# Attention in units of both heads and half a group's queries, the third score product on half the array's rows

## The chip, the cores and the metric

The kernel runs on one core of a Trainium2 chip. The time is the device time of one execution in microseconds (us). The engines of the core run side by side: TensorE (PE in the rows; its weight loads are a second row, PEld), VectorE (DVE), ScalarE (ACT), GpSimd (POOL), and SyncE (SP), which issues the DMAs. Matmuls write into PSUM, eight banks of 512 fp32 columns on 128 partitions; ACT and DVE read them from there.

## The reference

Two layers over 2048 tokens of width 1024. Layer 0 is a gated linear attention; layer 1, which the change touches, is a stick-breaking attention with 16 heads of 64 dimensions. Its core, per head and query:

```python
z = q @ k.T * scale                                   # keys strictly before the query
log_beta = log_sigmoid(z)
log_one_minus = where(strictly_before, log_beta - z, 0)
log_survive = cumsum(log_one_minus, reverse) - log_one_minus
weights = where(strictly_before, exp(log_beta + log_survive), 0)
o = (weights @ v) * silu(g) ; x + gate * (o @ w_out)
```

## The kernel before

All products are made in fp32r from a high and a low part of each operand, three matmuls for one product. Tokens lie in four groups of 512 (TG). Layer 0 takes the first 970 us or so of the span. Layer 1 runs over eight pairs of heads (p), and within a pair over the four query groups (g). For each pair and group `pair_linear` makes k, q, v and the gate g from the normed tokens (96 matmuls and more).

**Scores.** k holds, for each head, the high part in one half of the 128 partitions and the low part in the other. q's high part stands in both halves, so one 128-row matmul gives high times high and high times low (L821). The low part of q, also copied into both halves, gives the third product, with low times low for free (L822). Sigmoid of the scores on ACT (L825) gives 1 - beta; on a diagonal block POOL masks it (L827); a backward running product on DVE (L830) gives the survival of the stick, in S.

**Turns and values.** Four transposes (L838) bring a column block of S into a PSUM bank `pt`, of which there are two (pool `pw`). ACT takes the high part out of it (L841, `sh`), DVE the low part (L842, `sl`). Since S runs as a product, the values are multiplied as differences of neighbours, in high and low parts side by side (`v2`); two matmuls (L855, L856) add a turned block into the bank `o`. At the end `finish` adds the halves and multiplies by the gate.

**Units.** A unit is one head h, one query group g and one key group c (c from g down to 0). It has four steps: the four blocks of 128 queries for the scores, and the four blocks of 128 keys for turns and values. A diagonal unit (c = g) has shorter rows in both. TensorE's order is the order of the code (`manual_schedule`): at each step a score call, a share of the side work (`fill`: the next `pair_linear`, or the last projection), the values of a block turned three steps before, and the turn of a block whose scores began five steps before (LAG_T, LAG_V). The order on ACT and DVE is the scheduler's. The next pair's weights are scaled and split by ACT and DVE (`load_scaled`) during the third group of a pair and the fourth.

**q.** After its projection q's high part goes into half the partitions of `L.q` on ACT, one head at a time (L776, L777), its low part to `ql` on DVE (L778, L780), and four DMAs copy them into the other halves (L783, L784). 

The call that sets the order of the steps:

```python
u.scores(j)
turns.append((u, j))
step(fill, (i + 0.7) / len(steps))
if len(values) > LAG_V: ...          # values of an earlier turn
if len(turns) > LAG_T: ...           # a turn
```

Of the kernel before, what the change touches and what calls it, by code (L numbers as in the profile page):

```python
# [9 lines left out]
F32 = mybir.dt.float32  # L10
F32R = mybir.dt.float32r
AF = mybir.ActivationFunctionType
ALU = mybir.AluOpType
# [21 lines left out]
def yoco_kernel(ctx: ExitStack, tc: tile.TileContext, I: dict, O: dict):  # L35
# [696 lines left out]
    def pair_linear(p, g, W, Ls):  # L732
# [23 lines left out]
        else:  # L756
# [21 lines left out]
        nc.vector.scalar_tensor_tensor(L.ql[0][A], pq[A], bq[A], L.q[A, 0].bitcast(F32),  # L778
                                       op0=ALU.add, op1=ALU.subtract)
        nc.vector.scalar_tensor_tensor(L.ql[1][B], pq[B], bq[B], L.q[B, 1].bitcast(F32),  # L780
                                       op0=ALU.add, op1=ALU.subtract)
# [19 lines left out]
    class Unit:  # L801
# [6 lines left out]
        def __init__(self, p, g, h, c, Ls, before):  # L808
            self.p, self.g, self.h, self.c = p, g, h, c
            self.Ls, self.before = Ls, before  # L810
            self.diag = c == g
            self.n = f"{p}_{g}_{h}_{c}"
            self.S, self.split = [], []

        def scores(self, tb):
            L, h, diag = self.Ls[self.g], self.h, self.diag
            k = self.Ls[self.c].k
            w = (tb + 1) * P if diag else TG
# [4 lines left out]
            s_ = t2(f"S_{self.n}_{tb}")  # L823
            s = s_[:, 0:w]
            nc.scalar.activation(s, z, AF.Sigmoid, scale=-SCALE_B)  # L825
            if diag:
                nc.gpsimd.affine_select(s[:, w - P:], s[:, w - P:], pattern=[[-1, P]],  # L827
                                        compare_op=ALU.is_gt, fill=1.0, base=0, channel_multiplier=1)

            nc.vector.tensor_tensor_scan(s[:, ::-1], s[:, ::-1], s[:, ::-1],  # L830
                                       1.0 if diag else self.before.S[tb][:, 0:1], ALU.mult, ALU.min)
            self.S.append(s_)

        def turn(self, sb):
            t0 = sb if self.diag else 0
            pt = bank(pw, f"pt_{self.n}_{sb}")
            for tb in range(t0, 4):
                nc.tensor.transpose(pt[:, tb * P:(tb + 1) * P], self.S[tb][:, sb * P:(sb + 1) * P], ident)  # L838
            hi = t2(f"sh_{self.n}_{sb}", F32R)[:, t0 * P:]
            lo = t2(f"sl_{self.n}_{sb}", F32R)[:, t0 * P:]  # L840
            nc.scalar.activation(hi, pt[:, t0 * P:], AF.Copy, bias=-1.0)  # L841
            nc.vector.scalar_tensor_tensor(lo, pt[:, t0 * P:], -1.0, hi.bitcast(F32),  # L842
                                           op0=ALU.add, op1=ALU.subtract)
            self.split.append((hi, lo))

        def values(self, sb):
            if self.diag and sb == 0:
                self.o = bank(po, f"o_{self.n}")
            elif sb == 0:
                self.o = self.before.o  # L850
            t0 = sb if self.diag else 0
            o = self.o[:, t0 * P:]
            v = self.Ls[self.c].v[:, sb, self.h].rearrange("p a d -> p (a d)")
            hi, lo = self.split[sb]
            nc.tensor.matmul(o, v, hi, start=self.diag and sb == 0, stop=False)  # L855
            nc.tensor.matmul(o, v, lo, start=False, stop=self.c == 0 and sb == 3)  # L856
            if self.c == 0 and sb == 3:
                self.finish()

        def finish(self):  # L860
            p, g, h = self.p, self.g, self.h
            L = self.Ls[g]
            mine = slice(64 * h, 64 * h + 64)
            other = slice(64 - 64 * h, 128 - 64 * h)
            if h == 0:
                L.o = t2(f"oB_{p}_{g}")
            tmp = t2(f"ot_{p}_{g}_{h}")
            nc.scalar.activation(tmp[mine], self.o[other], AF.Copy)
            nc.vector.tensor_tensor(L.o[mine], self.o[mine], tmp[mine], op=ALU.add)  # L869
            if h == 1:  # L870
                nc.vector.tensor_tensor(L.o, L.o, L.g, op=ALU.mult)
# [60 lines left out]
    def layer1(after):  # L932
        Ls = {p: [] for p in range(SBP)}
        weave(pair_linear(0, 0, Ws[0], Ls[0]), (after, 0, 2))
        turns, values = [], []
# [28 lines left out]
        for p in range(SBP):  # L964
            for g in range(NG):
                units = []
                for h in range(2):
                    before = None
                    for c in range(g, -1, -1):
                        before = Unit(p, g, h, c, Ls[p], before)  # L970
# [102 lines left out]
```

## Time and profile before

| | |
|---|---|
| Time, median of 3 runs | 2706.01 us (2699.67 to 2706.11) |
| The profiled execution | 2703.88 us, of which the span of the program is 2702.1 us |
| TensorE busy | 2607.2 us, 96% of the span, 14040 matmuls |
| DVE busy | 2110.4 us, 78% |
| ACT busy | 1517.6 us, 56% |
| POOL busy | 167.4 us, 6% |
| DMA | 371.91 MB, 138 GB/s in the mean |

Busy times are unions of the instructions' times on one engine. A matmul's duration goes on after the next one has begun, so for TensorE the distance of two starts says what a matmul costs, and its duration says less. fp32 matmuls stand in the trace as two records each.

### The profile page before, as it was taken

The page shows a single profiled execution, that of the slowest core. Times are in us where ns is not written, and L with a number is a line of the kernel's source. Part 1 is how long each engine was busy: PE and PEld are TensorE (multiplying, and loading weights), DVE is VectorE, ACT ScalarE, POOL GpSimd, SP SyncE. Part 2 cuts the span into 40 slices and gives each one's busy share as a digit, 9 for nine tenths or more (in the row PEclk, how much of TensorE's full clock was granted, in tenths as well). Part 3 has the DMA queues.
Part 4 walks back from the last instruction along what each step waited for, and adds up shares of the span by engine and source line. Part 5 has one row for each costly group of instructions (what it writes and reads, how often), then busy time and mean ns, then how long its engine had stood idle before and what let it go on. Part 6 is the DMA issues. An engine that isn't in the chain of part 4 may idle for free.

```text
span 2702.1 us, 38165 instructions
## 1 busy us (share of the span) xinstructions
PE 2607.2 (96%) x14040; PEld 2184.4 (81%) x14040; DVE 2110.4 (78%) x2933; ACT 1517.6 (56%) x2677; POOL 167.4 (6%) x358
## 2 busy tenths in 40 slices
PE   5999999999999999999999999999999999999998
PEld 4888888888788878788787887887887887887887
DVE  7647767676675658978979969979879789789866
ACT  4746756574485445545545645546556555556644
POOL 3000000000000011000010010010000010010000
PEclk7999999999999999999999999999999999999999
DMA  6326445545732463342243334243243243323464
GB/s 246 118 74 209 151 151 175 168 148 173 232 131 72 164 247 127 106 145 90 96 146 116 114 107 154 88 137 116 75 148 110 72 151 113 115 93 117 148 212 147
DMA packets 116682, 371.91 MB, mean 138 GB/s; under 512 B 13872, under 2 KB 18096, under 8 KB 116496
## 3 DMA queue, kind: packets, MB, share of 16 engines
q1 hardware_dynamic: 116496, 369.47, 40.8%
q8 instruction: 111, 1.82, 0.3%
q14 instruction: 75, 0.61, 0.1%
HBM read 311.75 MB, written 40.89 MB: 131 GB/s over the span
## 4 chain that ended last, share of the span: by engine, by line
PE 75%; DVE 17%; ACT 3%; issue 3%; DMA 1%; POOL 0%; SPq 0%; DVEq 0%; POOLq 0%; ACTq 0%
PE pt L838 7%; DVE S L830 5%; PE z L822 4%; PE o L856 4%; PE z L821 4%; PE o L855 3%; DVE sl L842 3%; PE pg L150 2%; PE pg L152 2%; PE pg L151 2%; PE pf L150 2%; PE pf L151 2%; PE pf L152 2%; PE py L150 2%; PE lk L150 2%
## 5 line engine op out<-in xcount | busy, mean ns | idle before, releaser
L841 ACT ACTIVATE sh<-pt 128x512 fp32r<-128x512 f32 (+3 forms) x640 | 341.5, 534 | 531.7 <-PE pt L838 522.1
L842 DVE SCALAR_TENSOR_TENSOR sl<-pt,sh 128x512 fp32r<-128x512 f32 (+3 forms) x640 | 384.0, 601 | 163.5 <-ACT sh L841 157.6
L830 DVE TENSOR_TENSOR_SCAN S<-S,S 128x512 f32<-128x512 f32 x384 | 489.5, 1275 | 3.4 <-ACT S L825 3.0
L838 PE MATMUL pt<-ident,S 128*128 128x128 f32 x2176 | 346.9, 275 | 34.7 <-DVE sl L842 34.2
L838 PEld LDWEIGHTS pt<-ident,S 128*128 128x128 f32 x2176 | 266.1, 141 | 119.7 <-DVE sl L842 33.0
L825 ACT ACTIVATE S<-z 128x512 f32<-128x512 f32 (+3 forms) x640 | 339.5, 531 | 12.6 <-PE o L856 4.6
L821 PE MATMUL z<-k,q 128*128 128x512 f32 (+3 forms) x640 | 284.4, 444 | 0.0
L822 PE MATMUL z<-k,ql 128*128 128x512 f32 (+3 forms) x640 | 234.1, 366 | 0.9 <-DVE sl L842 0.5
L856 PE MATMUL o<-sl,v 128*128 128x512 f32 (+3 forms) x640 | 234.2, 366 | 0.0
L855 PE MATMUL o<-sh,v 128*128 128x512 f32 (+3 forms) x640 | 230.6, 360 | 0.0
L830 DVE TENSOR_TENSOR_SCAN S<-S 128x128 f32<-128x128 f32 (+3 forms) x256 | 209.3, 820 | 19.7 <-POOL S L827 16.7
L827 POOL TENSOR_SCALAR_AFFINE_SELECT S<-S 128x128 f32<-128x128 f32 x256 | 86.1, 337 | 1251.1 <-ACT S L825 1232.2
L444 PE MATMUL pv<-wh_v,h 128*128 128x256 f32 x512 | 155.0, 303 | 0.0
L446 PE MATMUL pv<-wh_v,h 128*128 128x256 f32 x512 | 145.3, 284 | 0.0
L445 PE MATMUL pv<-wl_v,h 128*128 128x256 f32 x512 | 145.2, 284 | 0.0
L855 PEld LDWEIGHTS o<-sh,v 128*128 128x128 f32 x640 | 120.6, 188 | 27.2
L856 PEld LDWEIGHTS o<-sl,v 128*128 128x128 f32 x640 | 120.6, 189 | 25.7
L821 PEld LDWEIGHTS z<-k,q 128*128 128x128 f32 x640 | 121.8, 190 | 5.5
L822 PEld LDWEIGHTS z<-k,ql 128*128 128x128 f32 x640 | 123.1, 192 | 1.5 <-DVE sl L842 0.7
L150 PE MATMUL pg<-h,wh_g 128*128 128x512 f32 x256 | 112.6, 440 | 0.0
L150 PE MATMUL lk<-xb,wh_w_kv 128*128 128x512 f32 x256 | 102.5, 400 | 7.6 <-DVE oB L869 7.6
L150 PE MATMUL lv<-xb,wh_w_kv 128*128 128x512 f32 x256 | 102.9, 402 | 3.5 <-DMA xb<-xn 3.5
(266 smaller groups left out, 6350.3 us busy)
## 6 DMA issues: line engine op xcount, KB each, us to landing
xb<-xn SPq DMA_DIRECT2D x256, 512.0 KB, 5.0
wa_l<-in_w_ada_dram SPq DMA_DIRECT2D x40, 512.0 KB, 5.2
wr_f<-in_w_out_dram SPq DMA_DIRECT2D x40, 512.0 KB, 3.8
x<-in_x_dram SPq DMA_DIRECT2D x32, 512.0 KB, 6.5
wr_v<-in_w_v_dram SPq DMA_DIRECT2D x32, 512.0 KB, 4.5
wr_kq<-in_w_kq_dram SPq DMA_DIRECT2D x32, 512.0 KB, 4.1
wr_g<-in_w_g_dram SPq DMA_DIRECT2D x32, 512.0 KB, 3.9
wr_out<-in_w_out_dram SPq DMA_DIRECT2D x32, 512.0 KB, 3.8
```

The costliest lines, as they stand in the source:

```text
L150: nc.tensor.matmul(out, hi, x[kt][0], start=first and i == 0, stop=False)
L444: nc.tensor.matmul(o, xh, hi, start=i == 0, stop=False)
L446: nc.tensor.matmul(o, xl, hi, start=False, stop=i == len(steps) - 1)
L821: nc.tensor.matmul(z, L.q[:, h, tcol], k[:, h, 0:w], start=True, stop=False)
L822: nc.tensor.matmul(z, L.ql[h][:, tcol], k[:, h, 0:w], start=False, stop=True)
L825: nc.scalar.activation(s, z, AF.Sigmoid, scale=-SCALE_B)
L830: nc.vector.tensor_tensor_scan(s[:, ::-1], s[:, ::-1], s[:, ::-1], 1.0 if diag else self.before.S[tb][:, 0:1], ALU.mult, ALU.min)
L838: nc.tensor.transpose(pt[:, tb * P:(tb + 1) * P], self.S[tb][:, sb * P:(sb + 1) * P], ident)
L841: nc.scalar.activation(hi, pt[:, t0 * P:], AF.Copy, bias=-1.0)
L842: nc.vector.scalar_tensor_tensor(lo, pt[:, t0 * P:], -1.0, hi.bitcast(F32), op0=ALU.add, op1=ALU.subtract)
L855: nc.tensor.matmul(o, v, hi, start=self.diag and sb == 0, stop=False)
L856: nc.tensor.matmul(o, v, lo, start=False, stop=self.c == 0 and sb == 3)
```

## The change

A unit is now both heads, half a query group (hf: 256 queries) and one key group.

- A score call takes 128 queries of both heads: two first products into two banks, then two third products. The third product of a head has only 64 rows: q's low part times k's high part, head 0 on array rows 0 to 63, head 1 on rows 64 to 127. It is called every second step, with two banks, two sigmoids and two scans; before, there was one of each at every step.
- A turned block has 128 keys, and both heads with 256 queries each. A value product is four matmuls, high and low for each head, of 256 columns. A diagonal unit of the first half has only two blocks of keys.
- q's high part is taken out of its bank in one operation of 128 partitions, its low part in another; four DMAs make `L.q`. There are no copies of the low part.
- A unit's end has two half-wide sums on ACT and DVE each, and half a gate, at the end of each half.

```diff
-        L.ql = [t2(f"ql{h}_{n}", F32R) for h in range(2)]
-        nc.scalar.activation(L.q[A, 0], pq[A], AF.Identity, bias=bq[A])
-        nc.scalar.activation(L.q[B, 1], pq[B], AF.Identity, bias=bq[B])
...
-        for x in (L.q[:, 0], L.q[:, 1]), L.ql:
-            nc.sync.dma_start(x[0][B].bitcast(F32), x[0][A].bitcast(F32))
-            nc.sync.dma_start(x[1][A].bitcast(F32), x[1][B].bitcast(F32))
+        qh, L.ql = t2(f"qh_{n}", F32R), t2(f"ql_{n}", F32R)
+        nc.scalar.activation(qh, pq, AF.Identity, bias=bq)
+        nc.vector.scalar_tensor_tensor(L.ql, pq, bq, qh.bitcast(F32), op0=ALU.add, op1=ALU.subtract)
+        for h, x in enumerate((A, B)):
+            for y in (A, B):
+                nc.sync.dma_start(L.q[y, h].bitcast(F32), qh[x].bitcast(F32))
...
-            z = bank(pz, f"z_{self.n}_{tb}")[:, 0:w]
-            nc.tensor.matmul(z, L.q[:, h, tcol], k[:, h, 0:w], start=True, stop=False)
-            nc.tensor.matmul(z, L.ql[h][:, tcol], k[:, h, 0:w], start=False, stop=True)
+            z = [bank(pz, f"z_{self.n}_{j}_{h}")[:, 0:w] for h in range(2)]
+            for h in range(2):
+                nc.tensor.matmul(z[h], L.q[:, h, tcol], k[:, h, 0:w], start=True, stop=False)
+            for h, rows in enumerate((A, B)):
+                nc.tensor.matmul(z[h], L.ql[rows, tcol], k[rows, h, 0:w], start=False, stop=True)
...
+            for h in range(2):
+                for j in range(f, 2):
+                    at = (2 * h + j) * P
+                    nc.tensor.transpose(pt[:, at:at + P], self.S[h, j][:, sb * P:(sb + 1) * P], ident)
...
-            nc.tensor.matmul(o, v, hi, start=self.diag and sb == 0, stop=False)
-            nc.tensor.matmul(o, v, lo, start=False, stop=self.c == 0 and sb == 3)
+            for h in range(2):
+                v = self.Ls[self.c].v[:, sb, h].rearrange("p a d -> p (a d)")
+                for i, x in enumerate(self.split[sb]):
+                    nc.tensor.matmul(self.o[:, h, f * P:], v, x[:, h], start=start and h == i == 0,
+                                     stop=stop and h == i == 1)
...
+            for h, (mine, other) in enumerate(((A, B), (B, A))):
+                nc.scalar.activation(tmp[mine], o[other, h], AF.Copy)
+                nc.vector.tensor_tensor(L.o[mine, cols], o[mine, h], tmp[mine], op=ALU.add)
+            nc.vector.tensor_tensor(L.o[:, cols], L.o[:, cols], L.g[:, cols], op=ALU.mult)
...
-                    u.scores(j)
-                    turns.append((u, j))
+                    if j % 2 == 0:
+                        u.scores(j // 2)
+                    sb = j + u.turns - 4
+                    if sb >= 0:
+                        turns.append((now + LAG_T, u, sb))
...
-                    if len(turns) > LAG_T:
-                        t = turns.pop(0)
+                    if turns and turns[0][0] <= now:
+                        t = turns.pop(0)[1:]
```

How the order changes is seen in the fourth pair (p = 3), at the last query group and its second key group (c = 2); in a name like `z_3_3_0_2_0` stand pair, group, head (now half), key group and step, then in the new one the head, and at the end a buffer number. TensorE before, one step: a score call, the values of one block, three matmuls of the next pair's projection, and the turn (four transposes):

```order
L821 MATMUL z_3_3_0_2_0_15883<-k_3_2_14940,q_3_3_15609 128x512
L822 MATMUL z_3_3_0_2_0_15883<-k_3_2_14940,ql0_3_3_15610 128x512
L855 MATMUL o_3_2_1_2_15675<-sh_3_2_1_0_0_15826,v2_3_0_14359 128x512
L856 MATMUL o_3_2_1_2_15675<-sl_3_2_1_0_0_15827,v2_3_0_14359 128x512
L150 MATMUL lv_4_0_15794<-xb_4_0_4_15786,wh_w_kv4_1_15648 128x512
L151 MATMUL lv_4_0_15794<-xb_4_0_4_15786,wh_w_kv4_1_15648 128x512
L152 MATMUL lv_4_0_15794<-xb_4_0_4_15786,wl_w_kv4_1_15649 128x512
L838 MATMUL pt_3_2_1_0_3_15897<-ident_86,S_3_2_1_0_0_15669 128x128
```

TensorE after, the first of two steps at the same place:

```order
L824 MATMUL z_3_3_0_2_0_0_16222<-k_3_2_15218,q_3_3_15929 128x512
L824 MATMUL z_3_3_0_2_0_1_16223<-k_3_2_15218,q_3_3_15929 128x512
L826 MATMUL z_3_3_0_2_0_0_16222<-k_3_2_15218,ql_3_3_15931 128x512
L826 MATMUL z_3_3_0_2_0_1_16223<-k_3_2_15218,ql_3_3_15931 128x512
L868 MATMUL o_3_2_1_2_16003<-sh_3_2_1_0_0_16161,v2_3_0_14641 128x256
L868 MATMUL o_3_2_1_2_16003<-sl_3_2_1_0_0_16162,v2_3_0_14641 128x256
L868 MATMUL o_3_2_1_2_16003<-sh_3_2_1_0_0_16161,v2_3_0_14641 128x256
L868 MATMUL o_3_2_1_2_16003<-sl_3_2_1_0_0_16162,v2_3_0_14641 128x256
L150 MATMUL lv_4_0_16136<-xb_4_0_4_16128,wh_w_kv4_1_15963 128x512
L151 MATMUL lv_4_0_16136<-xb_4_0_4_16128,wh_w_kv4_1_15963 128x512
L152 MATMUL lv_4_0_16136<-xb_4_0_4_16128,wl_w_kv4_1_15964 128x512
```

Two matmuls of 64 rows (L826) stand between full ones; the second step has the same values, projection and turn, and no scores.

DVE before, at the same place: evictions (L842) and scans (L830) by turns:

```order
L830 SCALAR_TENSOR_TENSOR S_3_3_0_2_1_15909<-S_3_3_0_2_1_15909,S_3_3_0_3_1_15810 128x512
L842 SCALAR_TENSOR_TENSOR sl_3_3_0_3_0_15923<-pt_3_3_0_3_0_15917,sh_3_3_0_3_0_15922 128x512
L830 SCALAR_TENSOR_TENSOR S_3_3_0_2_2_15929<-S_3_3_0_2_2_15929,S_3_3_0_3_2_15833 128x512
L842 SCALAR_TENSOR_TENSOR sl_3_3_0_3_1_15942<-pt_3_3_0_3_1_15937,sh_3_3_0_3_1_15941 128x384
L830 SCALAR_TENSOR_TENSOR S_3_3_0_2_3_15948<-S_3_3_0_2_3_15948,S_3_3_0_3_3_15863 128x512
```

DVE after:

```order
L835 SCALAR_TENSOR_TENSOR S_3_3_0_2_0_0_16228<-S_3_3_0_2_0_0_16228,S_3_3_0_3_0_0_16104 128x512
L835 SCALAR_TENSOR_TENSOR S_3_3_0_2_0_1_16231<-S_3_3_0_2_0_1_16231,S_3_3_0_3_0_1_16110 128x512
L854 SCALAR_TENSOR_TENSOR sl_3_2_1_0_3_16250<-pt_3_2_1_0_3_16244,sh_3_2_1_0_3_16249 128x512
L835 SCALAR_TENSOR_TENSOR S_3_3_0_2_1_0_16266<-S_3_3_0_2_1_0_16266,S_3_3_0_3_1_0_16171 128x512
L835 SCALAR_TENSOR_TENSOR S_3_3_0_2_1_1_16269<-S_3_3_0_2_1_1_16269,S_3_3_0_3_1_1_16177 128x512
```

The scans stand in twos now, one for each head, and the evictions between them.

## Rows read from the trace of the kernel before

**Rows 1.** The page's chain of work that ended last, by engine
```profile
PE 75%; DVE 17%; ACT 3%; issue 3%; DMA 1%; POOL 0%; SPq 0%; DVEq 0%; POOLq 0%; ACTq 0%
```

**Rows 2.** Busy us by stretch: PE, PEld, DVE, ACT, POOL; clock, DMA; third pair, groups 3, 4
```profile
1452.00:1509.00 57.00, 52.84 (x280) 42.15 (x278) 56.62 (x90) 36.28 (x74) 2.68 (x8) 1.00 0.38 125
1509.00:1588.00 79.00, 77.95 (x416) 65.42 (x417) 63.39 (x83) 39.81 (x77) 5.77 (x16) 1.00 0.27 81
```

**Rows 3.** The chain in time, one step of layer 1: start, us, engine, line
```profile
1501.80 0.23 PE z L821
1502.04 0.23 PE z L822
...
1503.43 0.44 PE pt L838 x4
1503.86 0.23 PE z L821
```

**Rows 4.** The chain in time, value matmuls of 384, 256 and 128 columns
```profile
1512.27 0.17 PE o L855
...
1514.22 0.12 PE o L855
...
1516.05 0.06 PE o L855
1516.11 0.11 PE o L856
```

**Rows 5.** Instructions by line and shape: count, busy us, mean ns of one
```profile
L822 PE MATMUL z<-k,ql 128*128 128x512 f32 x448 | 176.7, 395 | 0.0
```

**Rows 6.** Instructions in time, low-rank product of layer 0: start, us, engine, line
```profile
270.53 0.39 PE L152 MATMUL py<-og,wl_out 128*128 128x512 f32 x1
270.53 0.11 PEld L380 LDWEIGHTS plr<-h,lrw 128*32 128x32 f32 x1
...
270.75 0.40 PE L380 MATMUL plr<-h,lrw 128*32 128x512 f32 x1
```

**Rows 7.** TensorE in time, masked score block of layer 0
```profile
306.99 0.39 PE L474 MATMUL psc<-e,gk 128*128 128x128 f32 x2
307.30 0.33 PE L475 MATMUL psc<-e,kn 128*64 128x64 f32 x2
307.56 0.39 PE L444 MATMUL pv<-wh_v,h 128*128 128x256 f32 x1
307.78 0.28 PE L445 MATMUL pv<-wl_v,h 128*128 128x256 f32 x1
307.90 0.29 PE L446 MATMUL pv<-wh_v,h 128*128 128x256 f32 x1
```

**Rows 8.** Weight loads in time, same place
```profile
307.30 0.19 PEld L475 LDWEIGHTS psc<-e,kn 128*64 128x64 f32 x2
```

**Rows 9.** TensorE in time, fp32 matmuls on the full array in layer 0
```profile
316.96 0.60 PE L501 MATMUL po<-sc,v 128*128 128x128 f32 x4
317.40 0.60 PE L506 MATMUL pst<-v,kft 128*128 128x256 f32 x2
```

**Rows 10.** DVE's instructions by line and shape
```profile
L830 DVE TENSOR_TENSOR_SCAN S<-S,S 128x512 f32<-128x512 f32 x384 | 489.5, 1275 | 3.4 <-ACT S L825 3.0
L842 DVE SCALAR_TENSOR_TENSOR sl<-pt,sh 128x512 fp32r<-128x512 f32 x448 | 304.6, 680 | 145.1 <-ACT sh L841 140.9 <-PE pt L838 0.7 <-issue 0.7
L869 DVE TENSOR_TENSOR oB<-o,ot 64x512 f32<-64x512 f32 x64 | 43.5, 680 | 7.3 <-ACT ot L868 6.6
L842 DVE SCALAR_TENSOR_TENSOR sl<-pt,sh 128x256 fp32r<-128x256 f32 x64 | 26.6, 415 | 0.7
L778 DVE SCALAR_TENSOR_TENSOR ql<-lq,wbias,q 64x512 fp32r<-64x512 f32 x32 | 23.4, 730 | 3.6 <-ACT q L777 3.4
```

**Rows 11.** ACT's eviction of a turned block, third pair, by shape
```profile
L841 ACT ACTIVATE sh<-pt 128x512 fp32r<-128x512 f32 x56 | 33.5, 599 | 54.6 <-PE pt L838 54.2 <-PE z L821 0.3
```

**Rows 12.** TensorE's waits: for whom, us in total, times, longest
```profile
PE pt L838 <- DVE sl L842: 34.2, 55, 2.3
```

More of the change, by code (lines that the diff above doesn't have):

```diff
@@ L801, in yoco_kernel, with __init__ @@
     class Unit:
[L808 to L809 removed]
+        def __init__(self, p, g, hf, c, Ls, before):
+            self.p, self.g, self.hf, self.c = p, g, hf, c
             self.Ls, self.before = Ls, before
             self.diag = c == g
[L812 to L818, printed above, removed]
[L819 to L832 removed]
@@ L834, in turn, with first @@
+        def first(self, sb):
+            return max(0, sb - 2 * self.hf) if self.diag else 0
         def turn(self, sb):
-            t0 = sb if self.diag else 0
+            f = self.first(sb)
             pt = bank(pw, f"pt_{self.n}_{sb}")
[L837 to L844, printed above, removed]
+            for h in range(2):
+                for j in range(f, 2):
+                    at = (2 * h + j) * P
+                    nc.tensor.transpose(pt[:, at:at + P], self.S[h, j][:, sb * P:(sb + 1) * P], ident)
+            pt, hi, lo = (x.rearrange("p (h t) -> p h t", h=2)[:, :, f * P:] for x in
+                          (pt, t2(f"sh_{self.n}_{sb}", F32R), t2(f"sl_{self.n}_{sb}", F32R)))
@@ L846, in values @@
+            nc.scalar.activation(hi, pt, AF.Copy, bias=-1.0)
+            nc.vector.scalar_tensor_tensor(lo, pt, -1.0, hi.bitcast(F32), op0=ALU.add, op1=ALU.subtract)
+            self.split[sb] = hi, lo
         def values(self, sb):
-            if self.diag and sb == 0:
-                self.o = bank(po, f"o_{self.n}")
+            start = self.diag and sb == 0
+            stop = self.c == 0 and sb == self.turns - 1
+            if start:
+                self.o = bank(po, f"o_{self.n}").rearrange("p (h t) -> p h t", h=2)
@@ L849, in values @@
             elif sb == 0:
                 self.o = self.before.o
[L851 to L854, printed above, removed]
-            nc.tensor.matmul(o, v, hi, start=self.diag and sb == 0, stop=False)
-            nc.tensor.matmul(o, v, lo, start=False, stop=self.c == 0 and sb == 3)
-            if self.c == 0 and sb == 3:
+            f = self.first(sb)
+            for h in range(2):
+                v = self.Ls[self.c].v[:, sb, h].rearrange("p a d -> p (a d)")
+                for i, x in enumerate(self.split[sb]):
+                    nc.tensor.matmul(self.o[:, h, f * P:], v, x[:, h], start=start and h == i == 0,
+                                     stop=stop and h == i == 1)
@@ L872, in finish @@
+            if self.hf == 1:
                 if p < SBP - 1:
@@ L934, in layer1 @@
         weave(pair_linear(0, 0, Ws[0], Ls[0]), (after, 0, 2))
-        turns, values = [], []
+        turns, values, now = [], [], 0
         def final_all():
@@ L966, in layer1 @@
                 units = []
-                for h in range(2):
+                for hf in range(2):
                     before = None
                     for c in range(g, -1, -1):
-                        before = Unit(p, g, h, c, Ls[p], before)
+                        before = Unit(p, g, hf, c, Ls[p], before)
                         units.append(before)
```

38 lines of the change are left out of this document (24 added, 14 removed).

## The prediction

> **What bounds the kernel now.** I read the chain of work that ended last first: three quarters of the span is TensorE, DVE a sixth [rows 1]. So a change of TensorE's work counts where TensorE is the one that is late. The busy times by stage show where that is. In one pair's turn of the attention the stage of the last key group keeps TensorE busy for 77.95 of 79.00 us, with DVE at 63.39; in the stage before it DVE is busy for 56.62 of 57.00 us and TensorE for 52.84 [rows 2], because the next pair's weights are scaled on DVE there. So in each pair's turn 57 us belong to DVE, and TensorE has 57.00 - 52.84 = 4.2 us of idle there; the rest belongs to TensorE. The chain through one ordinary step shows the unit of account: seven 512-column products of 0.23 us and four transposes of 0.44 us, nothing between them [rows 3]. The granted clock is 1.00 in both stages [rows 2], the 2.4 GHz level, and stays so: TensorE doesn't fall idle in any case below.
>
> A matmul's own duration is not its price, since matmuls overlap: a 512-column one has a mean of 395 ns [rows 5] and costs 0.23 us of chain. I price by starts: 0.23 us at 512 columns, 0.17 at 384, 0.12 at 256, and for 128 the mean of 0.06 and 0.11, 0.085 [rows 3, 4].
>
> **The third product.** Before, there are 640 of them (448 with 512 columns [rows 5], and 64 for each smaller width): 448 x 0.23 + 64 x (0.17 + 0.12 + 0.085) = 127 us of chain. Now there are still 640, each 64 rows deep, as 320 pairs whose halves lie in different rows of the array and in different banks. If the halves run at the same time, a pair takes the time of one, and 127 / 2 = 63.5 us go. But TensorE now passes from the full array to two half arrays and back 320 times, and no row of before has a matmul on half the rows. The nearest rows disagree:
> - The low-rank product of layer 0 uses a 128 x 32 part of the array, between full matmuls of the same type (fp32r). Its weights are loaded at 270.53, as the full matmul ahead starts, and it starts 0.22 us after that one [rows 6]: the passage costs nothing.
> - The masked score block of layer 0 uses a 128 x 64 part, in fp32. The group begins at 306.99 and the second full matmul behind it at 307.78 [rows 7]. Less that first full matmul's 0.12, it holds TensorE for 0.67 us. Its work is one fp32 matmul of 128 columns and one of 64. Two fp32 matmuls of 128 columns (four records) take 317.40 - 316.96 = 0.44 us between full matmuls [rows 9], so this is worth 0.22 + 0.11 = 0.33. The other 0.34 us belong to the two passages. That it is the passage, not the type, is told by the weights: the load for the 64 columns doesn't start as soon as the matmul ahead runs, as the low-rank one does, but at 307.30, together with its own matmul [rows 7, 8].
>
> So the passages of a pair are bounded by 0 and 0.34 us, and from above once more by 0.11 us if the second half's weights can't be loaded beside the first's (loads in a row start 0.11 to 0.12 us apart, as the 256-column matmuls do that they feed [rows 7]). I take 0.34: that row shares the change's dimension, 64, and a group with two passages in it, while what it doesn't share, fp32, costs nothing at the passages between full matmuls [rows 9]. With it a pair costs 0.57 us for 512 columns in place of 0.46, and the whole is 224 x 0.57 + 32 x (0.17 + 0.12 + 0.085 + 3 x 0.34) = 172 us: **+45 us** in place of -63.5.
>
> The Trainium skill (TensorEngine Tiling (Array Packing), Key Properties) says that changing the tiling mode, not just the tile, drains TensorE. The 128 x 64 group agrees with it, with 0.34 us for two changes; the 128 x 32 rows do not, with none. By that rule the sum is the one above, without it the one of the first rival.
>
> **The values.** A value product covers both heads' halves separately now, so 512 columns become twice 256. In layer 0 a run of 256-column matmuls starts one every 0.12 us [rows 7], so two cost 0.24 for 0.23. Before: 2 x (448 x 0.23 + 64 x (0.17 + 0.12 + 0.085)) = 254 us; now 2048 x 0.12 + 256 x 0.085 = 268 us (by the loops: 48 places with c < g of 32 matmuls each, and 32 diagonals of 16 with 256 columns and 8 with 128). **+13 us**; +20 if each 128-column one costs 0.11. The transposes are the same 2176.
>
> **Where it lands.** Per pair the DVE-bound stage has 12 of the 40 score calls. Its share of the two terms is 9 x 0.11 + 0.17 + 0.22 + 0.26 = 1.6 and 0.5, together 2.1 us, less than TensorE's 4.2 us of idle there [rows 2], so I cost it at nothing for the seven pairs that prepare a next one: -15 us. If that cover were gone these 15 us would come back.
>
> **DVE and ACT.** Of two bias-and-split operations of 0.73 us on DVE one goes per group [rows 10]; the two sums of 0.68 us and the gate, as wide, become six of half the width, at 0.42 each [rows 10], +0.4; two short evictions fewer on the diagonal, about -0.3. Net -0.6 us per group, which counts only where DVE is the bound: 7 x 0.6 = **-4 us**. ACT has the same pattern and is at 36 us of 57 at most [rows 2]. The copies of q's high part are four DMAs per group on SP as before; 24 matmuls of the gate projection, 24 x 0.23 = 5.5 us, lie between them and the first score as now. The DMA waits of TensorE in the trace are not in this place.
>
> **A new burst on DVE.** The scans came one by one between evictions; now both heads' scans stand together, every second step. A turned block waits for ACT (0.60), then for up to two scans of 1.27, and its own 0.68: 3.8 us until its bank is free [rows 10, 11]. It was 2.55. There are two such banks, so the turn two steps later waits for it. Two steps last 4.1 us before (2 x 2.06, [rows 3]), and 4.25 in the forecast (2 x 0.23 + 0.57 + 8 x 0.12 + 6 x 0.23 + 8 x 0.11). So it mostly fits, with 0.4 us left. The same wait is 34.2 us of the span now [rows 12]. I add **10 us**, with 0 and 40 (some 130 blocks of two steps in the stages of the last key group, 0.3 us each) as its bounds.
>
> **Sum.** 45 + 13 - 15 - 4 + 10 = +49 us on the profiled execution's 2703.9 us: 2753. The median of the runs is 2706.0, 2 us above the profiled one, so I say **2754 us**. The bounds of this case alone: 320 x 0.11 = +35 for the second load, -10 to +30 for the burst, seldom both at their upper ends; some 2740 to 2800.
>
> **Rivals.**
> 1. *The passage costs nothing; not slower.* The low-rank rows [rows 6] are fp32r, as here. Then -63.5 + 13 = -50; the DVE-bound stage's share, (2.45 - 0.5) x 7 = 14, isn't had; -4; +10: -30 us, 2673 to 2676. It decides from a passage cost per pair below (63.5 - 13) / 320 = 0.16 us. For it: same type, a load seen ahead of its turn. Against it: the 64-wide group. The Trainium skill (TensorE: Matmul & The Clock Gate, The mechanism) states that matmuls on different row groups overlap, and that loads for them do; no row here shows two matmuls side by side. 2655 if the DVE-bound stage gains too.
> 2. *The gain is there and DVE's burst eats it.* Without passage costs two steps shrink to 2 x 0.23 + 0.23 + 0.96 + 1.38 + 0.88 = 3.9 us, against 3.8 us of a turned block's way [rows 10, 11] and 2 x (1.27 + 0.68) = 3.9 us of DVE's own work. Then the turn waits in most blocks, and the 40 us bound is paid: 2690 to 2712, no change.
> 3. *The halves don't overlap, and the passage is free.* The change then does not do what it says: 0 for the third product, +13 - 3 - 4 + 10: about 2720, slower.
> 4. *Neither overlaps and the passage is paid.* The forecast and 63.5 us more, less the other 2.1 us of idle in seven pairs: 2754 + 63 - 15, about 2802.
>
> **How the numbers follow.** Forecast 0.47; rival 1 0.33; rival 2 0.09; rival 3 0.06; rival 4 0.05. A difference under 0.3%, 8 us, can't be told from none here. Faster by more: rival 1 but for its edge, and a little of rival 2: 0.36. Within: most of rival 2 and the edges of its neighbours: 0.10. Slower: 0.54. The range must hold the forecast and rival 1: 2662 to 2790 leaves out rival 4 and the tails, about 0.15 to 0.2. The forecast's own range is 2740 to 2800.
>
> **What would show it.** In the profile after, the gap between the start of a second score product and the start of the next full matmul: 0.23 + 0.23 us if the passage is free and the halves overlap, 0.23 + 0.57 in the forecast; the starts of the two halves' matmuls, a few ns apart or 0.11 or 0.23; whether the weights behind them are loaded before or after the pair's end. For the values, starts 0.12 us apart. For the burst, the sum of what the transposes wait for DVE's evictions, 34 us now. The stage of the third key group should stay at 57 us in any case. I am wrong if the pair costs under 0.4 us of chain, or if the DVE-bound stage moves as much as the others.

## The result, and the profile after

The changed kernel takes 2767.95 us in the median (2766.66 to 2770.13), the kernel before beside it 2704.28: a ratio of 1.0238, 95% interval 1.0223 to 1.0253, so some 64 us slower. The forecast was 2754, slower, with a range of 2662 to 2790.

The page of after: its span, TensorE's busy time, and the chain of work that ended last, by engine.

```profile
span 2765.5 us, 39915 instructions
...
PE 2680.4 (97%) x15064; PEld 2185.8 (79%) x15064; DVE 2094.7 (76%) x2933; ACT 1502.3 (54%) x2645; POOL 186.9 (7%) x358
...
PE 78%; DVE 14%; ACT 3%; DMA 3%; issue 1%; SPq 0%; DVEq 0%; ACTq 0%
```

TensorE is busy for 73 us more than before, in 1024 more matmuls, and its share of the chain rose from 75% [rows 1] to 78%. DVE is busy for 16 us less. So the added time stands in TensorE's row; what it is made of, the experiments below take apart.

Where it came is seen by stages. These are busy times of the stretch from one query group's first score matmul to the next one's, for the four groups of the fourth pair. The columns are as in [rows 2]. First the kernel before:

```profile
1556.70:1588.60 31.90, 31.90 (x164) 26.57 (x162) 17.70 (x24) 11.98 (x24) 3.70 (x10) 1.00 0.25 69
1588.60:1628.20 39.60, 39.60 (x213) 33.25 (x212) 32.27 (x44) 20.39 (x41) 4.06 (x10) 1.00 0.49 168
1628.20:1683.00 54.80, 51.99 (x281) 42.39 (x279) 51.72 (x81) 34.82 (x71) 3.71 (x10) 1.00 0.34 114
1683.00:1749.80 66.80, 64.37 (x354) 53.28 (x352) 64.83 (x88) 39.71 (x78) 3.57 (x10) 1.00 0.32 105
```

The same pair after:

```profile
1580.60:1612.10 31.50, 31.50 (x166) 25.56 (x165) 15.31 (x22) 9.83 (x21) 5.04 (x10) 1.00 0.20 62
1612.10:1654.80 42.70, 42.59 (x241) 34.12 (x240) 32.14 (x45) 20.88 (x43) 5.25 (x10) 1.00 0.46 159
1654.80:1712.40 57.60, 55.56 (x322) 43.02 (x320) 52.71 (x84) 35.03 (x73) 3.64 (x10) 1.00 0.34 113
1712.40:1782.10 69.70, 67.60 (x409) 53.31 (x408) 64.35 (x85) 39.24 (x76) 4.01 (x10) 1.00 0.30 100
```

One pair's turn rose from 193.1 to 201.5 us. The second, third and fourth stages rose by about 3 us each. The third stage, the one in which TensorE has idle time, rose like the others. The granted clock is 1.00 in all of them.

Now one score call, in the fourth pair. TensorE first:

```profile
1604.48 0.40 PE L152 MATMUL lq<-xb,wl_w_qg 128*128 128x512 f32 x1
1604.71 0.62 PE L824 MATMUL z<-k,q 128*128 128x512 f32 x2
1605.27 0.49 PE L826 MATMUL z<-k,ql 64*128 64x512 f32 x2
1605.69 0.51 PE L150 MATMUL lg<-xb,wh_w_qg 128*128 128x512 f32 x1
1606.03 0.40 PE L151 MATMUL lg<-xb,wh_w_qg 128*128 128x512 f32 x1
1606.27 0.40 PE L152 MATMUL lg<-xb,wl_w_qg 128*128 128x512 f32 x1
```

The weight loads of the same place:

```profile
1604.48 0.42 PEld L824 LDWEIGHTS z<-k,q 128*128 128x128 f32 x2
1605.26 0.19 PEld L826 LDWEIGHTS z<-k,ql 64*128 64x128 f32 x2 [0.36 <-issue]
1605.69 0.19 PEld L150 LDWEIGHTS lg<-xb,wh_w_qg 128*128 128x128 f32 x1 [0.24 <-issue]
1605.80 0.19 PEld L151 LDWEIGHTS lg<-xb,wh_w_qg 128*128 128x128 f32 x1
```

Three things can be read there.

- **The halves run side by side.** Both L826 matmuls together last 0.49 us, and one of them alone has a mean of 0.496. By their records they start 3 ns apart (the median of 320 pairs; 4 ns at most). The Trainium skill (TensorE: Matmul & The Clock Gate, The mechanism) says that matmuls on different row groups overlap, and their loads too: this trace agrees.
- **The way in is paid.** A full matmul's weights are loaded while the matmul ahead runs: L824's at 1604.48, with L152. Those of the halves are loaded at 1605.26, together with their own matmuls, after a gap of 0.36 us in which the load path has nothing.
- **The way out is paid.** The next full matmul's weights are loaded at 1605.69, again together with their own matmul, and the one behind it starts 0.34 us later in place of 0.23.

From the first L824 to the L151 it is 1606.03 - 1604.71 = 1.32 us. Five full matmuls of 512 columns, the first three products and two behind them, would be 5 x 0.23 = 1.15. The forecast's 0.57 for a pair, with three full matmuls, would have made it 3 x 0.23 + 0.57 = 1.26; it is a little more.

What the transposes wait for DVE, which was 34.2 us [rows 12]:

```profile
PE pt L850 <- DVE sl L854: 31.5, 34, 1.5
```

The wait did not grow. Before the experiments I therefore put the whole 64 us down to the passages and the split values. That did not hold.

### The profile page after: what moved, and what is told of

Same layout as the page of the kernel before. It is cut to its first block, busy times and chain, and to the rows that moved or that the text cites. A ratio compares the mean times of both kernels' runs of the same rounds, so it can differ in the third digit from the quotient of the medians.

```text
span 2765.5 us, 39915 instructions
## 1 busy us (share of the span) xinstructions
PE 2680.4 (97%) x15064; PEld 2185.8 (79%) x15064; DVE 2094.7 (76%) x2933; ACT 1502.3 (54%) x2645; POOL 186.9 (7%) x358
## 4 chain that ended last, share of the span: by engine, by line
PE 78%; DVE 14%; ACT 3%; DMA 3%; issue 1%; SPq 0%; DVEq 0%; ACTq 0%
PE o L868 8%; PE pt L850 7%; DVE S L835 4%; PE z L824 4%; PE z L826 4%; PE lv L150 2%; PE pg L150 2%; PE lk L150 2%; DVE sl L854 2%; PE pf L150 2%; PE pg L152 2%; PE pg L151 2%; PE pf L151 2%; PE pf L152 2%; PE lq L150 2%; PE lv L152 2%
## 5 line engine op out<-in xcount | busy, mean ns | idle before, releaser
L853 ACT ACTIVATE sh<-pt 128x512 fp32r<-128x512 f32 x576 | 329.2, 573 | 447.2 <-PE pt L850 438.9
L854 DVE SCALAR_TENSOR_TENSOR sl<-pt,sh 128x512 fp32r<-128x512 f32 x576 | 372.3, 654 | 148.0 <-ACT sh L853 140.4
L830 ACT ACTIVATE S<-z 128x512 f32<-128x512 f32 (+3 forms) x640 | 308.1, 533 | 128.1 <-PE z L826 112.6
L868 PE MATMUL o<-sh,v 128*128 128x256 f32 (+1 forms) x1152 | 300.3, 284 | 0.0
L868 PE MATMUL o<-sl,v 128*128 128x256 f32 (+1 forms) x1152 | 297.1, 280 | 0.0
L868 PEld LDWEIGHTS o<-sh,v 128*128 128x128 f32 x1152 | 216.9, 188 | 32.3 <-issue 7.4
L868 PEld LDWEIGHTS o<-sl,v 128*128 128x128 f32 x1152 | 217.5, 189 | 22.0
L824 PE MATMUL z<-k,q 128*128 128x512 f32 (+3 forms) x640 | 205.6, 400 | 2.1 <-DMA q<-qh 1.3
L826 PE MATMUL z<-k,ql 64*128 64x512 f32 (+3 forms) x640 | 149.3, 462 | 0.0
L826 PEld LDWEIGHTS z<-k,ql 64*128 64x128 f32 x640 | 59.6, 183 | 95.6 <-issue 89.0
L150 PE MATMUL lg<-xb,wh_w_qg 128*128 128x512 f32 x256 | 115.2, 450 | 0.0
L150 PE MATMUL lq<-xb,wh_w_qg 128*128 128x512 f32 x256 | 114.6, 448 | 0.0
```

What stands on the lines that cost most here:

```text
L150: nc.tensor.matmul(out, hi, x[kt][0], start=first and i == 0, stop=False)
L824: nc.tensor.matmul(z[h], L.q[:, h, tcol], k[:, h, 0:w], start=True, stop=False)
L826: nc.tensor.matmul(z[h], L.ql[rows, tcol], k[rows, h, 0:w], start=False, stop=True)
L830: nc.scalar.activation(s, z[h], AF.Sigmoid, scale=-SCALE_B)
L853: nc.scalar.activation(hi, pt, AF.Copy, bias=-1.0)
L854: nc.vector.scalar_tensor_tensor(lo, pt, -1.0, hi.bitcast(F32), op0=ALU.add, op1=ALU.subtract)
```

## The experiments

Two measures are used below. The time is that of the runs. The table at the end of this section has **waits by starts**: how much later than usual the first transpose of a block starts after the matmul ahead of it (more than 0.23 us after a matmul of 512 columns, more than 0.12 after one of 256). This is more than the trace's own sum of waits, because a matmul's duration covers the first part of a wait.

### One part at a time

**One head's half product alone (e2_half_alone).** The kernel before, its third product cut to 64 rows and nothing else:

```diff
-            nc.tensor.matmul(z, L.ql[h][:, tcol], k[:, h, 0:w], start=False, stop=True)
+            rows = B if h else A
+            nc.tensor.matmul(z, L.ql[h][rows, tcol], k[rows, h, 0:w], start=False, stop=True)
```

> The kernel before with the third product of each head on 64 rows, one at a time: 640 passages in and out instead of none, and no second half beside it. Theory: each costs 0.40 us (two passages of about 0.105 for the drain and 0.107 for a weight load that can't be hidden), 640 x 0.40 = 256 us, a little less for the idle time it fills: 2930 to 2960 us. Rival: the passages are cheap and the depth of a matmul alone changes nothing: 2704 us.

Measured: 2882.82 us (2880.71 to 2886.68), a ratio of 1.0672 [1.0656, 1.0687]. That is +180 us, 0.28 for each of the 640 half products, and less than the 2930 to 2960 expected. TensorE in time, one of them:

```profile
1603.99 0.48 PE L821 MATMUL z<-k,q 128*128 128x512 f32 x1
1604.40 0.49 PE L823 MATMUL z<-k,ql 64*128 64x512 f32 x1
1604.83 0.50 PE L150 MATMUL lg<-xb,wh_w_qg 128*128 128x512 f32 x1
1605.17 0.40 PE L151 MATMUL lg<-xb,wh_w_qg 128*128 128x512 f32 x1
```

A score call of the kernel before, in the stage of the third group:

```profile
1503.62 0.48 PE L821 MATMUL z<-k,q 128*128 128x512 f32 x1
1503.93 0.39 PE L822 MATMUL z<-k,ql 128*128 128x512 f32 x1
1504.17 0.39 PE L855 MATMUL o<-sh,v 128*128 128x512 f32 x1
1504.40 0.40 PE L856 MATMUL o<-sl,v 128*128 128x512 f32 x1
```

From the first product to the second matmul behind the third product it is 1.18 us with the half, 0.78 without: 0.40 with 512 columns. In the medians of all calls it is 0.39 for 256 columns and more, 0.28 for 128, and 0.38 in the mean of the 640; over five pairs of heads, by the turns, 0.37. The time shows only 0.28 because the waits of TensorE for DVE go: those by starts fall from 5.4 us per pair of heads to none, and the wait of `lk` for `oB` (1.3 us by starts) goes too; in the kernel before that one is

```profile
PE lk L150 <- DVE oB L869: 7.6, 7, 1.1
```

Together this is (5.4 + 1.3) x 8 = 54, and (180 + 54) / 640 = 0.37. So the passage is real, and its price is that of the rows above.

**Columns instead of rows (e4_cols64).** Is it narrowness as such? The low-rank product of layer 0, which uses 32 of the array's columns [rows 6], was given 64 columns, in fp32r, over all 128 rows; one of its eight blocks keeps 32:

```diff
-            nc.tensor.matmul(pr[0:32], lrw[:, kt], T.hs[kt][0], start=kt == 0, stop=False)
...
+            n = 32 if T.g == 0 or kt == 7 else 64
+            w = flat[:, 32 * kt:32 * kt + n]
+            nc.tensor.matmul(pr[0:n], w, T.hs[kt][0], start=i == 0, stop=False)
...
```

> A look at the passages alone. In layer 0's low-rank product (groups 1 to 3) 64 columns of weights in place of 32 for all but one of the eight steps, the further 32 columns being other weights whose results nobody reads; that one step keeps 32 columns. All in fp32r. Before, 128 x 32 parts are entered and left at no cost. If the 64-wide part is what must be passed into and out of, the load in front of a 64-column matmul begins some 0.3 us after the full matmul ahead has begun, as at the half-depth pairs, and the same between 64 and 32 columns or not; if fp32 was what cost it in the masked score block, every load begins a few ns after the matmul ahead, and the starts stay 0.23 us apart. The time is that of the kernel before, within 2 us.

Measured: 2703.72 us, a single run. TensorE in time, into the narrow product:

```profile
270.47 0.40 PE L152 MATMUL py<-og,wl_out 128*128 128x512 f32 x1
270.70 0.39 PE L383 MATMUL plr<-h,lrw 128*64 128x512 f32 x1
270.93 0.39 PE L384 MATMUL plr<-h,lrw 128*64 128x512 f32 x1
271.16 0.40 PE L383 MATMUL plr<-h,lrw 128*32 128x512 f32 x1
```

Its weight loads:

```profile
270.47 0.13 PEld L383 LDWEIGHTS plr<-h,lrw 128*64 128x64 f32 x1
270.70 0.13 PEld L384 LDWEIGHTS plr<-h,lrw 128*64 128x64 f32 x1
270.93 0.11 PEld L383 LDWEIGHTS plr<-h,lrw 128*32 128x32 f32 x1
```

Each load begins with the matmul ahead, and all starts lie 0.23 us apart, from 128 to 64 columns and from 64 to 32. So using fewer columns costs nothing in fp32r, at 64 as at 32, in these rows. The Trainium skill (TensorEngine Tiling (Array Packing), Key Properties) says that a change of the tiling mode drains TensorE: the half rows of the experiment before agree, with 0.38 us for the way in and out; these rows show no drain at all.

**The values alone (e5_split).** The kernel before, with its value products in pieces of at most 256 columns:

```diff
-            nc.tensor.matmul(o, v, hi, start=self.diag and sb == 0, stop=False)
-            nc.tensor.matmul(o, v, lo, start=False, stop=self.c == 0 and sb == 3)
...
+            for a in range(0, n, 256):
+                e = min(n, a + 256)
...
+                nc.tensor.matmul(o[:, a:e], v, hi[:, a:e], start=first, stop=False)
+                nc.tensor.matmul(o[:, a:e], v, lo[:, a:e], start=False, stop=last)
```

> The kernel before with each value product in pieces of at most 256 columns, nothing else. The prediction's term: 896 products of 512 columns become two of 256 at 0.12 us in place of one of 0.23, +0.01 each, 9 us, and the 128 of 384 columns 256 + 128 at 0.12 + 0.085 for 0.17, +4 us: +13 us, 2717 us. If TensorE's idle time beside DVE takes some of it, 2712. If the halving is free, 2704.

Measured: 2714.8 us (2709.97 to 2718.26), ratio 1.0045 [1.0031, 1.0058]: +12 us, as expected.

**One of the two halves (e6_one_half).** The changed kernel with head 1's half product left out, so that each call goes to the half array and back for one matmul:

```diff
-            for h, rows in enumerate((A, B)):
-                nc.tensor.matmul(z[h], L.ql[rows, tcol], k[rows, h, 0:w], start=False, stop=True)
+            nc.tensor.matmul(z[0], L.ql[A, tcol], k[A, 0, 0:w], start=False, stop=True)
...
```

> The changed kernel with head 1's half-depth third product left out, head 0's kept on its 64 rows (head 1's scores lack that term). In the trace of the changed kernel the two halves start 3 ns apart. If they run side by side, leaving one out changes nothing: 2768 us, within 0.3%. If the second adds its 0.23 us after all, this kernel is some 60 us faster: 2705 us.

Measured: 2754.55 us (2754.36 to 2756.06), 13 less than the changed kernel, and so outside the 0.3% that was expected. On TensorE the second half is all but free: with 512 columns the next projection matmul starts 0.423 us (median) after a half alone, 0.429 after a pair. The 13 us are in the waits by starts, 4.3 us per pair of heads in place of 5.7, which is 11 over eight pairs. What shortens them was not tried.

### The units without the half depth

**The changed kernel with third products of full depth (e1_full)**, that is, the units of both heads alone:

```diff
-            for h, rows in enumerate((A, B)):
-                nc.tensor.matmul(z[h], L.ql[rows, tcol], k[rows, h, 0:w], start=False, stop=True)
+            for h in range(2):
+                nc.tensor.matmul(z[h], L.ql[h][:, tcol], k[:, h, 0:w], start=False, stop=True)
```

with q's preparation as before the change.

> The changed kernel with the third products of full depth again (q's low part copied into both halves, as before); units, order and values stay changed. Theory: the passages between the full and the half array cost the time. In the trace of the changed kernel a pair of 512 columns costs 0.64 us of chain where two full ones cost 0.46 (0.18 more, 224 times), and 0.24 to 0.35 more at the smaller widths (32 times each): 67 us in all. So this kernel should take 2768 - 67 = 2701 us, 2697 to 2708. Rival: the units of both heads (two scans in a row, twice as many value products, another order) cost it, and the half-deep pair is a gain of up to 63 us; then this kernel is at 2768 or above, up to 2830.

Measured: 2752.31 us (2750.55 to 2754.43), ratio 1.0187 [1.0172, 1.0202]. Neither theory had expected it: the units cost about 50 us without any passage, and the half depth only 16 more. TensorE's waits:

```profile
PE pt L854 <- DVE sl L858: 62.3, 72, 2.4
...
PE z L830 <- DMA ql<-ql: 7.1, 10, 2.1
```

The transposes wait for DVE twice as long as before or after. The second row is a smaller part: the copies of q's low part, which the changed kernel does without, come late ten times. With q's preparation as before, DVE also has one operation of 0.73 us more in each group than the changed kernel [rows 10]; what of the 62 us hangs on that was not tried.

**Head 1's third product left out of that (e3_one_full).** This stands for halves side by side with a free passage, the first rival of the prediction:

```diff
-            for h in range(2):
-                nc.tensor.matmul(z[h], L.ql[h][:, tcol], k[:, h, 0:w], start=False, stop=True)
+            nc.tensor.matmul(z[0], L.ql[0][:, tcol], k[:, 0, 0:w], start=False, stop=True)
```

> The changed kernel with full-depth third products, and head 1's left out (so head 1's scores lack the term of q's low part). TensorE has then the work that the change would have left it if two halves side by side cost one product and the passages nothing. Theory (TensorE sets the time, and DVE has room): 63.5 us less than the full-depth version, less what falls into the stretches where DVE is the bound (TensorE waits 5 us of a pair's 193 for DVE, in one stretch of some 35 us): 2640 to 2655 us. Rival (the scans that come in twos eat the gain): 2690 to 2712 us, with the transposes' waits for DVE's evictions at 70 us or more, from 31.5.

Measured: 2702.51 us (2699.69 to 2706.11), ratio 1.0003 [0.9994, 1.0012], no change against before. In time this is the rival's; the waits are 62 us rather than the 70 that it wanted:

```profile
PE pt L853 <- DVE sl L857: 61.7, 65, 2.1
```

So a free passage would not have made the kernel faster in this form.

A part of that is the clock. These are the third and fourth stage of the fourth pair, and two stretches of its third stage, with the columns of [rows 2]:

```profile
1626.80:1683.90 57.10, 52.71 (x309) 44.69 (x308) 53.41 (x82) 35.44 (x73) 3.63 (x10) 0.97 0.36 131
1683.90:1751.40 67.50, 63.87 (x395) 55.20 (x394) 64.38 (x89) 40.26 (x77) 4.14 (x10) 0.97 0.29 91
1672.00:1676.30 4.30, 2.28 (x14) 1.84 (x13) 4.24 (x8) 0.81 (x3) 0.00 (x0) 1.00 0.84 267
1676.30:1679.70 3.40, 3.40 (x14) 2.91 (x13) 3.34 (x5) 2.81 (x7) 0.00 (x0) 0.50 0.97 333
```

TensorE was busy for 2.28 of 4.30 us, and then ran at the 1.2 GHz level for 3.4 us. From 1015 us of the span to the last score call this run has ten such stretches, 34 us together, each right behind a transpose's wait for DVE of 2.0 to 2.1 us; the kernel before has two with 7 us, the changed kernel none. By an estimate from these rows half of the 27 us between them, some 14 us of the lost gain at most, is the lower clock that came behind the waits.

**Full depth, one head's scores per call (e10_one_head).** Units, values and turned blocks stay as in e1_full; but a call makes the scores of block j // 2 for head j % 2 alone, so that the two scans no longer come together:

```diff
...
-                    if j % 2 == 0:
-                        u.scores(j // 2)
+                    u.scores(j)
```

> The full-depth form in units of both heads, but each score call again makes the scores of one head only, at every step, as before; the turns come at the same steps. So DVE's scans are issued one by one again, and the units, the value products and the turned blocks stay those of both heads. Theory (the 50 us of the full-depth form are for the most part the transposes' wait behind two scans at a time): their wait for DVE falls from 62 us to 40 or less and the time from 2752 to 2715 to 2725. Rival (the 50 us belong to the units, the value products and the turned blocks of both heads): 2740 or more, the wait stays at 55 or more.

Measured: 2722.85 us (2721.64 to 2724.96), ratio 1.0069 [1.0054, 1.0084]; the transposes' waits:

```profile
PE pt L852 <- DVE sl L856: 45.9, 57, 2.2
```

Of the 50 us 30 are gone. By the starts 22 of them are the transposes' waits (9.8 to 7.0 us per pair of heads), so the two scans in a row make the larger part of the 35 us of waits that the units add. The trace's wait for the transposes did not fall to the 40 us expected. The waits by starts fell in the fourth group's stage, from 5.2 to 2.4 us per pair of heads, and not in the third's (4.6 in both).

### DVE's load

**The weights' running sum on GpSimd (e8_before_pool, e9_after_pool, e11_one_pool).** To relieve DVE in the third and fourth stages, the same edit was made in the kernel before, the changed one, and e3_one_full:

```diff
...
-                        nc.vector.scalar_tensor_tensor(acc, raw[:, j], s, acc, op0=ALU.mult, op1=ALU.add)
+                        nc.gpsimd.tensor_scalar(raw[:, j], raw[:, j], s, None, op0=ALU.mult)
+                        nc.gpsimd.tensor_tensor(acc, acc, raw[:, j], op=ALU.add)
```

> The kernel before, with the running sum of the scaled weights (the acc of load_scaled, 128 operations of 0.33 to 0.48 us on DVE, 7.3 us for each pair of heads) made on GpSimd instead, as a product in place and a sum. Theory (the transposes wait for DVE because the weights' scaling fills it in the stages of the third and fourth group): their wait falls from 34 us to 15 or less, and the time from 2704 to 2680 to 2690. Rival (the wait comes from the order of a block's steps on DVE, not from its load, or GpSimd's operations slow DVE's): 2698 or more.

> The changed kernel with the same edit. By the starts in the trace its transposes wait 5.7 us for each pair of heads, all in the stages of the third and fourth group. Theory: most of that goes, 2768 to 2730 to 2745, and what is left over the relieved kernel before is the price of the passages, about 50 us. Rival (the wait is not a matter of DVE's load): 2760 or more.

> The full-depth form without head 1's third product (it stands for halves side by side and a free passage; the output lacks that product), with the same edit. Without the edit it took 2702.5 and its transposes waited 10.8 us for each pair of heads by their starts. Theory (the gain of a free passage was lost to DVE, which is full): 2650 to 2670. Rival (DVE's load does not matter, the two scans in a row do): 2695 or more.

Measured: 2751.25, 2831.31 and 2772.37 us, all three slower than without the edit, by 47, 63 and 70. They do not answer the question, since the edit brought a wait of its own. DVE's waits in e9_after_pool, the second longest of them:

```profile
DVE S L836 <- POOL S L833: 100.0, 32, 7.9
```

S is masked on GpSimd in diagonal blocks, and the masks now stand behind the weights' operations in GpSimd's queue: DVE's scans wait for them up to 7.9 us at a time (3.8 in the changed kernel), and TensorE's transposes up to 9.1 us. The granted clock fell there too, to 0.50 for 10.2 us in the fourth pair's third stage. (GpSimd takes 1.2 to 1.6 us for the product and 0.8 to 0.9 for the sum; DVE took 0.47 for both. DVE's own durations did not change: its scan has a mean of 1275 ns in e8_before_pool as in [rows 10].)

**The running sum left out (e12_after_noacc, e13_before_noacc).** So the same operations were taken away without a substitute:

```diff
                     if kt == 0:
                         nc.vector.tensor_scalar(acc, raw[:, j], s, None, op0=ALU.mult)
-                    else:
-                        nc.vector.scalar_tensor_tensor(acc, raw[:, j], s, acc, op0=ALU.mult, op1=ALU.add)
```

> The changed kernel without seven of each eight operations of the weights' running sum (14 of 0.47 us on DVE for each pair of heads, 6.6 us; the bias of the projections then lacks seven of eight parts). Nothing takes their place on another engine. Theory (the transposes' waits, 5.7 us for each pair of heads by their starts, come from DVE's load in the stages of the third and fourth group): they fall below 2 us and the time from 2768 to 2730 to 2745. Rival (they come from the order of a block's steps, the two scans before an eviction): 2758 or more.

> The kernel before with the same operations left out. Theory: its transposes' waits, 4.1 us for each pair of heads by their starts, fall below 1.5 us and the time from 2704 to 2675 to 2688; what then lies between the two relieved kernels, some 50 to 60 us, is the price on TensorE alone, the passages and the value products. Rival: 2696 or more, and the distance between the two stays at 64.

Measured: the changed kernel 2733.7 us (2731.13 to 2733.97), 34 less; the kernel before 2667.88 us (2664.89 to 2668.33), 34 to 36 less. The transposes' waits, the changed kernel first:

```profile
PE pt L848 <- DVE sl L852: 7.9, 13, 1.3
```

```profile
PE pt L836 <- DVE sl L840: 15.6, 20, 2.1
```

By the starts they are 1.1 and 2.0 us per pair of heads, in place of 5.7 and 5.4 (below 1.5 had been expected of the kernel before). So the waits are for the larger part a matter of DVE's load in both kernels. But the distance between the two is 65.8 us, where 50 to 60 had been expected, about the same as between the whole kernels, 63.7. With DVE relieved the change costs what it costs with DVE full.

The stages and waits of all forms, worked out from the starts in the traces; us for each pair of heads, the mean of the second to the sixth pair:

```
                    stage 1  stage 2  stage 3  stage 4   turn   waits by starts
                                                                stage 3  stage 4
before                31.9     39.6     54.8     66.8   193.1     3.6      1.8
after                 31.5     42.7     57.5     69.8   201.5     3.1      2.6
e1_full               30.6     41.6     56.8     69.9   198.9     4.6      5.2
e3_one_full           30.0     39.3     56.5     67.4   193.2     5.8      5.0
e10_one_head          30.5     40.8     56.8     66.6   194.8     4.6      2.4
e6_one_half           31.4     42.8     56.6     68.8   199.7     2.4      1.9
e5_split              32.1     39.9     55.7     66.6   194.3     4.2      1.5
e2_half_alone         34.8     45.6     60.0     76.0   216.4     0.0      0.0
e13_before_noacc      31.9     39.6     51.2     65.5   188.2     0.4      1.6
e12_after_noacc       31.5     42.8     54.4     68.0   196.6     0.3      0.8
```

## Why the prediction held, and where it did not

The direction was right and the time lies in the range, 14 us above the forecast. The step that decided was the passage, and it was there. The terms, over eight pairs, from the starts (8.4 us a turn make 67 us, a little over the 64 us of the times, since the last pair prepares no next one):

**The third product: +45 forecast, about +60 measured.** Against the same units with full depth (e1_full), a score call with the matmul behind it takes, by the medians, 0.173 us more with 512 columns, 0.21 with 384, 0.27 with 256 and 0.175 with 128: 224 x 0.173 + 32 x 0.66 = 60, 0.19 for each of the 320 calls. The halves side by side give back 0.20 us in the mean of all widths (the second L830 of e1_full costs that, and 3 ns now), and the passages take 0.20 + 0.19 = 0.39; e2_half_alone has 0.38. The forecast had 0.34, near in size, but by luck, since its reason was wrong: I took the masked score block because it "shares the change's dimension, 64" [rows 7]. Its 64 are columns, and 64 columns cost nothing in fp32r (e4_cols64). What makes that fp32 block pay was not tried. The better reason would have been that neither row uses half the rows, and that the bound of 0 had then no better claim than the bound of 0.34.

**The values: +13 forecast, +14 measured.** This is e1_full against the kernel before, without the waits. About 9 of these come with the pieces alone (e5_split). The other 5 come with the new order, and what they are was not separated. The rest of TensorE's work in e1_full is some 2 us less than before, transposes 5 more and the others 7 less; it had no term in the forecast.

**The cover in the DVE-bound stage: -15 forecast, about nothing.** This is the step that failed: "so I cost it at nothing", and "The stage of the third key group should stay at 57 us in any case." It rose by 2.8 us for each pair of heads, like its neighbours, and by the prediction's own sign ("if the DVE-bound stage moves as much as the others") it was wrong there. I had read DVE's 56.62 of 57.00 us and TensorE's 4.2 us of idle [rows 2] as a stage that DVE sets from end to end. With DVE relieved, the stage takes 51.2 us before and 54.4 after, 3.1 more; with DVE full 2.8 of these show. The waits before were 3.6 us, and after they are still 3.1.

**The burst of two scans: +10 forecast within 0 and 40; 35 in e1_full, 2 in the changed kernel.** In e1_full the waits by starts are 9.8 us for each pair of heads, 5.4 before: 4.4 x 8 = 35. e10_one_head shows that most of it is the two scans together. In the changed kernel the waits are 5.7, +0.3 x 8 = 2; TensorE is held up by passages there, which, as I read it, leaves DVE time; DVE's lighter preparation of q may have a share. So the idle time did take in work, 4.1 x 8 = 33 us of it, but it was idle time that the change itself had made. With the copies of q's low part that e1_full waits for, 0.8 x 8 = 6 us, this is why the half depth, 60 us of TensorE's own time, adds only 16 to e1_full. Together the last two terms were -5 in the forecast and are +2: errors of 15 and 8 us, one each way. Both came from pricing the burst and the cover apart, where they are one wait of the same instructions.

**DVE's edits: -4 forecast; one wait of 10 us went.** The wait of `lk` for `oB`, 7.6 us in the trace's sum and 1.3 for each pair of heads by starts, is gone in the changed kernel. It is gone in e1_full too, which has q's old preparation, so it belongs to the halved ends of units or to the order, not to q; which of the two was not tried. In e13_before_noacc, with the old ends and order, it is gone with DVE's load.

60 + 14 - 2 + 2 - 10 = 64 us, where the turns give 67. So 3 us are in no term. The miss of 14 us is, within 2, the passage and the cover, each forecast 15 too low, less 8 for the burst and 6 for DVE's edits, forecast too high.

**The rivals.** The first, a free passage with 2673 to 2676, is out by the rows of the pair. But it had also been priced wrongly: e3_one_full has no passage at all and takes 2702.5. There the second rival is what happens, the gain eaten by DVE, with its price of 2690 to 2712 and its bound of 40 us: (5.8 + 5.0 - 5.4) x 8 = 43. There "TensorE doesn't fall idle in any case below" did not hold either: the granted clock fell ten times. So the second rival deserved the first one's chance, and the 0.36 for faster was too high. The third and fourth are out, since the halves start 3 ns apart.

Of the forms that leave nothing out, none came out faster than the kernel before; the best in units of both heads, e10_one_head, is 0.7% slower.

## What to carry to other kernels

Half the array's rows, as a pair between full matmuls, don't pay: a pair saved 0.20 us here, and going there and back cost 0.39. By these prices it would take more than two pairs in a row to gain clearly, which no run here tried; look for such runs. Idle time of an engine that waits for another is no cover to be spent beforehand; ask whether the change also alters the order on the engine waited for, and price wait and cover as one. When two engines are both near full, the trial that tells is to take work off one of them, and to take it away rather than to move it into a queue that others wait for.

## What was not expected of the hardware

- A matmul on half the rows costs more than one on all of them, if it stands alone between full ones: 0.23 + 0.39 = 0.62 us of TensorE in place of 0.23, with 512 columns (e2_half_alone).
- Half of the rows costs a passage and, in fp32r, half of the columns does not: loads of 128 x 64 and 128 x 32 begin with the matmul ahead, as full ones do, while loads of 64 x 128 begin with their own matmul (e4_cols64 and the changed kernel).
- The passage stands on both sides. On the way out the next full weights are loaded only when their matmul can start, and the matmul behind is 0.34 us away in place of 0.23.
- Waits of 2 us can be followed by a lower clock: in e3_one_full TensorE was busy for 2.28 of 4.30 us, and the granted clock was then 0.50 for 3.4 us; this came ten times in layer 1.
